# Another order of the seven down products, with one token half complete after the fifth

## The chip, the cores and the metric

One core of a Trainium2 chip. The engines named below are TensorE (PE), VectorE (DVE), ScalarE (ACT), GpSimd (POOL) and SyncE (SP), which here issues nearly all DMA transfers. The metric is the device time of one execution in microseconds.

## The reference, cut to what matters

Two layers on 1024 tokens of 1024 features (FF width 2816). Each layer is a mixer, a layer norm, a SwiGLU feed-forward and another layer norm:

```
def layer_norm(x, g, b):
    xf = x.astype(jnp.float32)
    mu = jnp.mean(xf, -1, keepdims=True)
    var = jnp.mean(jnp.square(xf - mu), -1, keepdims=True)
    return ((xf - mu) * lax.rsqrt(var + LN_EPS)).astype(x.dtype) * g + b

def swiglu(x, w_gate, w_up, w_down):
    return (jax.nn.silu(x @ w_gate) * (x @ w_up)) @ w_down
...
        x = layer_norm(ALPHA * x + mix, ln_mix_g[l], ln_mix_b[l])
        x = layer_norm(ALPHA * x + swiglu(x, ffn_w_gate[l], ffn_w_up[l], ffn_w_down[l]),
                       ln_ffn_g[l], ln_ffn_b[l])
```

The mixer of layer 0 is attention, that of layer 1 retention and a spatial-gating MLP; its first step (`gate`) multiplies the transposed output of layer 0 by a weight slice.

## The kernel before

**Matrix products in seven.** Each large product of the feed-forward is cut in two along tokens, features and the inner dimension, and done with seven half-size products in place of eight, on sums and differences of the blocks. For the down projection, product i (1 to 7) multiplies operand `h_ops[i-1]`, which the gate/up stage has stored to DRAM, by a block of `ffn_w_down` (i = 1, 2, 4) or by a stored combination `d_ops` (i = 3, 5, 6, 7). The results are added into `y[0]` and `y[1]`, the rows of the two token halves (4 row blocks of 128 tokens each, 1024 features in two column halves `ca` and `cb`). In the order of the kernel before: product 1 begins half 0, `ca`; 2 completes that; 6 and 5 begin half 1 (`ca`, `cb`); 7 completes half 1, `cb`, and begins half 0, `cb`; 3 completes half 1, `ca`; 4 completes half 0, `cb`. Products 1, 6, 7, 4 use one set of four PSUM banks (`side` true), 2, 5, 3 another, of which two banks come from the pool `trp` that the transposes use too.

**Precision.** Each operand tile is split into a rounded high part (a cast on ACT, L66) and a remainder (a subtraction on DVE, L67), and each 128x128 by 128x512 step is three matmuls (high by high, high by low, low by high). A product has 11 inner steps k, 4 row blocks b4 and 3 passes, 132 matmuls; a layer's down stage 924. Products run k by k over all row blocks, but the last one (i = 4) runs row block by row block after its first k.

**Buffers.** Operands come through four raw buffers of 512 KB (`load_raw`, `raw_h` and `raw_d`), h tiles through a pool of 11, weights through `w_unit`: unit `turn[0] % n` is one of eight tiles of the lasting pool `wpool`, or, from 8 on, a tile of an extra pool: four (`fw`) in the gate/up stage, six (`fww`) in the down stage. The pools of the down stage use the memory that the gate/up stage's pools (`c0`, `fw`) leave, so a tile in them waits until those have been read for the last time.

**Order.** The kernel is scheduled by its framework's list scheduler, which decides the order of each engine's queue; only the mixers' PE order is written out. Each engine, and SP's queue, works in order.

**After the products.** `sum_up` adds a product's PSUM to `y`; when a row block is complete `rows_done` normalises it, stores it (`scratch`, or `out` in layer 1) and, in layer 0, transposes it (`row_to_x`, L148) and splits it into the next layer's operand `xn`: with `pe` the remainder is made by a matmul with the negative identity and a copy on ACT (L153, L154), else by a subtraction on DVE (L156). `layer_norm` with `act` normalises on ACT (L174), multiplies on DVE (L175) and adds on POOL (L176); else two instructions on DVE do it (L178, L179). The reciprocal root is a pow on POOL (L166). The sums are L1040 and L1044; `zps` (L127) is the gate's product, `oq0ps` (L117) the first product behind it, `bw_u` (L872) the last product of gate/up, and `cy` and `c0` the results there, stored by L1009.

Of the kernel before, what the change touches and what calls it, by code (L numbers as in the profile page):

```python
# [11 lines left out]
F32 = mybir.dt.float32  # L12
# [6 lines left out]
P = 128  # L19
# [3 lines left out]
NB = SEQ // P  # L23
# [12 lines left out]
def tile_trunk(  # L36
# [7 lines left out]
    V, A, G, T, S = nc.vector, nc.scalar, nc.gpsimd, nc.tensor, nc.sync  # L44
# [5 lines left out]
    small = ctx.enter_context(tc.tile_pool(name="small", bufs=4))  # L50
# [19 lines left out]
    turn = [0, 0]  # L70
# [84 lines left out]
        else:  # L155
            V.tensor_sub(xt[:, :, 1, sl], ps, xt[:, :, 0, sl].bitcast(F32))  # L156

    def ln_stats(src, n, name):
        st = small.tile([P, n, 6], F32, tag="st", name=f"st_{name}")
        for j in range(n):  # L160
            V.bn_stats(st[:, j], src[:, j * 512:(j + 1) * 512])
        mv = small.tile([P, 2], F32, tag="mv", name=f"mv_{name}")
        V.bn_aggr(mv, st.rearrange("p a b -> p (a b)"))
        rstd = small.tile([P, 1], F32, tag="rstd", name=f"rstd_{name}")
        V.tensor_scalar_add(rstd, mv[:, 1:2], EPS)
        G.tensor_tensor(rstd, rstd, nhalf[:, 0:1], op=ALU.pow)  # L166
        return mv, rstd

    def layer_norm(row, gb, n, name, act=False):
        mv, rstd = ln_stats(row, n, name)  # L170
        if act:
            nm = small.tile([P, 1], F32, tag="c", name=f"nm_{name}")
            V.scalar_tensor_tensor(nm, mv[:, 0:1], -1.0, rstd, op0=ALU.mult, op1=ALU.mult)
            A.activation(row, row, AF.Identity, bias=nm, scale=rstd)  # L174
            V.tensor_mul(row, row, gb[0])  # L175
            G.tensor_add(row, row, gb[1])  # L176
        else:
            V.scalar_tensor_tensor(row, row, mv[:, 0:1], gb[0], op0=ALU.subtract, op1=ALU.mult)  # L178
            V.scalar_tensor_tensor(row, row, rstd, gb[1], op0=ALU.mult, op1=ALU.add)  # L179
# [444 lines left out]
    def odd_mixer(xT, zw0, res):  # L624
        with ExitStack() as st:
# [38 lines left out]
            def gate():  # L664

                zw = [zw0, col2_w(w_in, 2304, "zv1")]
                for g in (0, 1):
                    for t in range(NB):
                        ps = mm_tile("zps")
                        yield from gemm_R(ps[:, :256], zw[g], xT[t // 4], t % 4)  # L670
                        if g == 0:
                            A.copy(zv[:, t, :256], ps[:, :256])
                        else:
                            A.activation(zv[:, t, 256:], ps[:, :256], AF.Gelu_apprx_tanh)
                            A.activation(zv[:, t, :256], zv[:, t, :256], AF.Gelu_apprx_tanh)
                            layer_norm(zv[:, t], lngb, 1, f"sgu{t}")
                        yield 0.33
# [172 lines left out]
    def rest(layer, op, ahead=None):  # L850
# [7 lines left out]
        with ExitStack() as st:  # L858
# [156 lines left out]
            with ExitStack() as sl:  # L1015
# [7 lines left out]
                d_src = {1: wd[:, 0, :, ca], 2: wd[:, 1, :, ca], 4: wd[:, 1, :, cb], 6: d_ops[0][:, :, ca],  # L1023
                         7: d_ops[0][:, :, cb], 3: d_ops[1][:, :, ca], 5: d_ops[1][:, :, cb]}

                def rows_done(h, b4):
                    yt = y[h][:, b4]
                    t = 4 * h + b4
                    layer_norm(yt, gb, 2, f"f{layer}{h}{b4}")
                    if last:  # L1030
                        S.dma_start(out[0, t * P:(t + 1) * P, :], yt)
                    else:
                        S.dma_start(scratch[t], yt)
                        for c in (0, 1):
                            row_to_x(yt[:, c * 512:(c + 1) * 512], xn[h][c], b4, trp, f"f{layer}{h}{b4}{c}")

                def sum_up(i, b4, ps):
                    def first(h, c):
                        yt = y[h][:, b4, c]
                        V.scalar_tensor_tensor(yt, yt, ALPHA, ps, op0=ALU.mult, op1=ALU.add)  # L1040

                    def more(h, c, op=V.tensor_add):
                        yt = y[h][:, b4, c]
                        op(yt, yt, ps)  # L1044

                    if i == 1:
                        first(0, ca)
                    elif i == 2:
                        more(0, ca)
                    elif i == 6:  # L1050
                        first(1, ca)
                    elif i == 5:
                        first(1, cb)
                    elif i == 7:
                        more(1, cb)
                        first(0, cb)
                    elif i == 3:
                        more(1, ca)
                        rows_done(1, b4)
                    else:  # L1060
                        more(0, cb, V.tensor_sub)
                        rows_done(0, b4)

                bank = {}
                for i in (1, 2, 6, 5, 7, 3, 4):
                    end = i == 4
                    if end and not last:
                        loaded = ahead()
                        turn[0] = 4
                    if i == 3 and not last:  # L1070
                        xn = new_x("xn")
                    hs, ds = [], []
                    for q in range(0, NP, 2):
# [33 lines left out]
                    else:  # L1107
# [2 lines left out]
                                part(k, b4)  # L1110
                        for b4 in range(4):
                            sum_up(i, b4, bank[side][b4])
                more_w.pop()
            more_r.pop()
            return None if last else (xn, loaded, scratch)
# [51 lines left out]
```

## Time and profile before

| | |
|---|---|
| time, median of 3 runs | 2332.98 us (2329.07 to 2333.74) |
| the profiled execution | 2331.5 us |
| its span | 2329.6 us |
| mean granted clock of PE | 0.989 |
| PE busy, share of the span | 97% |
| DVE, ACT, POOL busy | 65%, 39%, 5% |
| down-stage matmuls (`pd`, L1096) | 1848, 427.2 us busy |

The span is that of the profile, from the first instruction to the end of the last; the time of the execution is 1.9 us longer. Busy shares are means over the whole span; a place where an engine waits shows only in the waits, the windows and the timeline.

### The profile page before, as it was taken

The page shows a single profiled execution, that of the slowest core. Times are in us where ns is not written, and L with a number is a line of the kernel's source. Part 1 is how long each engine was busy: PE and PEld are TensorE (multiplying, and loading weights), DVE is VectorE, ACT ScalarE, POOL GpSimd, SP SyncE. Part 2 cuts the span into 40 slices and gives each one's busy share as a digit, 9 for nine tenths or more (in the row PEclk, how much of TensorE's full clock was granted, in tenths as well). Part 3 has the DMA queues.
Part 4 walks back from the last instruction along what each step waited for, and adds up shares of the span by engine and source line. Part 5 has one row for each costly group of instructions (what it writes and reads, how often), then busy time and mean ns, then how long its engine had stood idle before and what let it go on. Part 6 is the DMA issues. An engine that isn't in the chain of part 4 may idle for free.

```text
span 2329.6 us, 30375 instructions
## 1 busy us (share of the span) xinstructions
PE 2262.2 (97%) x11372; PEld 1881.6 (81%) x11372; DVE 1506.2 (65%) x3030; ACT 904.2 (39%) x1740; POOL 108.5 (5%) x103
## 2 busy tenths in 40 slices
PE   8999999999999999989998999999999999989997
PEld 6888888878788888868886988888788888877885
DVE  4767676777877667755558523446976766755557
ACT  4545455553543333334332321122543333334431
POOL 0000000001200000000002100001200000000001
PEclk9999999999999999999998999999999999999998
DMA  5212121224254545457555111144344445457553
GB/s 168 68 46 59 42 58 40 70 90 136 87 190 163 170 152 164 147 195 268 199 186 173 42 46 46 46 149 149 123 148 159 159 162 169 137 197 270 172 193 123
DMA packets 195538, 312.36 MB, mean 134 GB/s; under 512 B 14784, under 2 KB 98368, under 8 KB 195392
## 3 DMA queue, kind: packets, MB, share of 16 engines
q1 hardware_dynamic: 195392, 310.44, 40.5%
q8 instruction: 89, 1.46, 0.3%
q14 instruction: 57, 0.47, 0.1%
HBM read 218.64 MB, written 87.56 MB: 131 GB/s over the span
## 4 chain that ended last, share of the span: by engine, by line
PE 78%; DVE 11%; DMA 7%; ACT 2%; issue 2%; POOL 0%; SPq 0%; POOLq 0%; ACTq 0%; DVEq 0%
PE bx_g L872 8%; PE bx_u L872 7%; PE pd L1096 7%; PE bw_g L872 5%; PE bw_u L872 5%; PE vps L127 4%; PE qps L117 4%; PE kps L117 3%; PE po_o L231 3%; DMA raw_d<-d_ops 3%; PE bv_g L872 3%; PE bv_u L872 2%; PE bz_u L872 2%; PE bz_g L872 2%; PE zps L127 2%; PE ovps L127 2%
## 5 line engine op out<-in xcount | busy, mean ns | idle before, releaser
L1096 PE MATMUL pd<-w_d,h 128*128 128x512 f32 x1848 | 427.2, 394 | 19.9 <-ACT w_d L66 15.0
L1096 PEld LDWEIGHTS pd<-w_d,h 128*128 128x128 f32 x1848 | 351.1, 190 | 95.5 <-ACT w_d L66 15.9
L872 PE MATMUL bx_g<-xs,w_g 128*128 128x512 f32 x792 | 192.2, 390 | 0.6 <-ACT w_g L66 0.6
L872 PE MATMUL bx_u<-xs,w_u 128*128 128x512 f32 x792 | 190.9, 389 | 0.0
L67 DVE TENSOR_TENSOR w_d<-raw_d,w_d 128x512 fp32r<-128x512 f32 x154 | 100.4, 685 | 124.5 <-ACT w_d L66 124.4
L872 PEld LDWEIGHTS bx_g<-xs,w_g 128*128 128x128 f32 x792 | 148.2, 188 | 32.2 <-ACT w_g L66 0.8
L872 PEld LDWEIGHTS bx_u<-xs,w_u 128*128 128x128 f32 x792 | 148.6, 188 | 30.8
L66 ACT CAST w_d<-raw_d 128x512 fp32r<-128x512 f32 x154 | 88.7, 618 | 147.4 <-DMA raw_d<-d_ops 101.4
L67 DVE TENSOR_TENSOR h<-raw_h,h 128x512 fp32r<-128x512 f32 x154 | 102.5, 684 | 58.4 <-ACT h L66 58.4
L872 PE MATMUL bw_u<-xs,w_u 128*128 128x512 f32 x528 | 130.9, 390 | 3.4 <-DVE cy L923 3.4
L872 PE MATMUL bw_g<-xs,w_g 128*128 128x512 f32 x528 | 130.7, 389 | 0.0
L66 ACT CAST h<-raw_h 128x512 fp32r<-128x512 f32 x154 | 91.6, 618 | 93.2 <-DMA raw_h<-h_ops 92.4
L872 PEld LDWEIGHTS bw_u<-xs,w_u 128*128 128x128 f32 x528 | 99.0, 188 | 24.8 <-DVE cy L923 4.3
L437 ACT ACTIVATE s<-s,mx 128x640 f32<-128x640 f32 (+7 forms) x128 | 93.2, 731 | 65.4 <-DVE mx L435 65.0
L127 PE MATMUL vps<-w_v,x 128*128 128x256 f32 x768 | 115.0, 294 | 1.5 <-DVE k L337 1.5
L872 PEld LDWEIGHTS bw_g<-xs,w_g 128*128 128x128 f32 x528 | 99.0, 188 | 20.5
L117 PE MATMUL qps<-x,w_q 128*128 128x512 f32 x384 | 109.9, 408 | 0.9 <-ACT w_q L66 0.9
L117 PE MATMUL kps<-x,w_k 128*128 128x512 f32 x384 | 110.4, 408 | 0.0
L127 PEld LDWEIGHTS vps<-w_v,x 128*128 128x128 f32 x768 | 101.3, 194 | 6.5 <-issue 4.6
L66 ACT CAST w_u<-raw_u 128x512 fp32r<-128x512 f32 x118 | 73.2, 622 | 78.9 <-issue 41.5
L67 DVE TENSOR_TENSOR w_u<-raw_u,w_u 128x512 fp32r<-128x512 f32 x118 | 80.8, 686 | 35.6 <-ACT w_u L66 35.4
L66 ACT CAST w_g<-raw_g 128x512 fp32r<-128x512 f32 x110 | 68.3, 625 | 87.8 <-PE bw_g L872 37.5
(574 smaller groups left out, 4070.5 us busy)
## 6 DMA issues: line engine op xcount, KB each, us to landing
raw_h<-h_ops SPq DMA_DIRECT2D x70, 512.0 KB, 4.1
h_ops<-cy SPq DMA_DIRECT2D x110, 256.0 KB, 3.1
raw_g<-in_ffn_w_gate_dram SPq DMA_DIRECT2D x44, 512.0 KB, 4.5
raw_u<-in_ffn_w_up_dram SPq DMA_DIRECT2D x44, 512.0 KB, 5.1
raw_dr<-in_ffn_w_down_dram SPq DMA_DIRECT2D x44, 512.0 KB, 3.6
d_ops<-raw_dr SPq DMA_DIRECT2D x44, 512.0 KB, 2.7
raw_d<-d_ops SPq DMA_DIRECT2D x40, 512.0 KB, 5.0
raw_d<-in_ffn_w_down_dram SPq DMA_DIRECT2D x30, 512.0 KB, 4.7
```

Source lines behind the costliest of these rows:

```text
L66: A.copy(dst[:, 0], src)
L67: V.tensor_sub(dst[:, 1], src, dst[:, 0].bitcast(F32))
L117: T.matmul(ps, w[k // 4][:, a, (k % 4) * P:(k % 4 + 1) * P], xh[k // 4][:, k % 4, b, :], start=n == 0, stop=n == 3 * KT - 1)
L127: T.matmul(ps, xh[k // 4][:, k % 4, a, b4 * P:(b4 + 1) * P], ws[k // 2][:, b, (k % 2) * 256:(k % 2) * 256 + 256], start=n == 0, stop=n == ...
L231: T.matmul(ps, self.xo[h][c][:, k, a, b4 * P:(b4 + 1) * P], self.w[c][2 * nh + k // 2][k % 2][:, b], start=n == 0, stop=n == 11)
L437: A.activation(s[:, :L], s[:, :L], AF.Exp, bias=self.mx[:, m:m + 1], scale=0.125, accum_out=self.sm[:, m:m + 1])
L872: T.matmul(ps, w[:, a, k * P:(k + 1) * P], X[i][:, k, b, :], start=first and n == 0, stop=n == 11, skip_group_check=more or not first)
L1096: T.matmul(bank[side][b4], hs[k][:, a, b4 * P:(b4 + 1) * P], ds[k][:, b], start=fresh and k == 0 and n == 0, stop=k == NP - 1 and n == 2, ...
```

## The change

The seven down products run in the order 1, 5, 6, 3, 7, 2, 4. Half 1 is complete with the fifth of them (product 7), and its four row blocks are normalised after that product, with `act` and, in layer 0, transposed with `pe`. Half 0 is still complete with product 4, but its `ca` half already with product 2, so the first of its two `bn_stats` is taken there and copied later (`st0`). `turn[0]` is set to 0 ahead of the products, so that product 1 begins with the units of `wpool`. The gate of layer 1's mixer takes the row blocks of half 1 first.

```diff
@@ -155,9 +155,12 @@
         else:
             V.tensor_sub(xt[:, :, 1, sl], ps, xt[:, :, 0, sl].bitcast(F32))
 
-    def ln_stats(src, n, name):
-        st = small.tile([P, n, 6], F32, tag="st", name=f"st_{name}")
-        for j in range(n):
+    def ln_stats(src, n, name, st=None):
+
+        s0, st = st, small.tile([P, n, 6], F32, tag="st", name=f"st_{name}")
+        if s0 is not None:
+            V.tensor_copy(st[:, 0], s0)
+        for j in range(s0 is not None, n):
             V.bn_stats(st[:, j], src[:, j * 512:(j + 1) * 512])
         mv = small.tile([P, 2], F32, tag="mv", name=f"mv_{name}")
         V.bn_aggr(mv, st.rearrange("p a b -> p (a b)"))
@@ -166,8 +169,8 @@
         G.tensor_tensor(rstd, rstd, nhalf[:, 0:1], op=ALU.pow)
         return mv, rstd
 
-    def layer_norm(row, gb, n, name, act=False):
-        mv, rstd = ln_stats(row, n, name)
+    def layer_norm(row, gb, n, name, act=False, st=None):
+        mv, rstd = ln_stats(row, n, name, st)
         if act:
             nm = small.tile([P, 1], F32, tag="c", name=f"nm_{name}")
             V.scalar_tensor_tensor(nm, mv[:, 0:1], -1.0, rstd, op0=ALU.mult, op1=ALU.mult)
@@ -665,7 +668,7 @@
 
                 zw = [zw0, col2_w(w_in, 2304, "zv1")]
                 for g in (0, 1):
-                    for t in range(NB):
+                    for t in (4, 5, 6, 7, 0, 1, 2, 3):
                         ps = mm_tile("zps")
                         yield from gemm_R(ps[:, :256], zw[g], xT[t // 4], t % 4)
                         if g == 0:
@@ -1023,16 +1026,18 @@
                 d_src = {1: wd[:, 0, :, ca], 2: wd[:, 1, :, ca], 4: wd[:, 1, :, cb], 6: d_ops[0][:, :, ca],
                          7: d_ops[0][:, :, cb], 3: d_ops[1][:, :, ca], 5: d_ops[1][:, :, cb]}
 
+                st0 = {}
+
                 def rows_done(h, b4):
                     yt = y[h][:, b4]
                     t = 4 * h + b4
-                    layer_norm(yt, gb, 2, f"f{layer}{h}{b4}")
+                    layer_norm(yt, gb, 2, f"f{layer}{h}{b4}", act=h == 1, st=None if h else st0[b4])
                     if last:
                         S.dma_start(out[0, t * P:(t + 1) * P, :], yt)
                     else:
                         S.dma_start(scratch[t], yt)
                         for c in (0, 1):
-                            row_to_x(yt[:, c * 512:(c + 1) * 512], xn[h][c], b4, trp, f"f{layer}{h}{b4}{c}")
+                            row_to_x(yt[:, c * 512:(c + 1) * 512], xn[h][c], b4, trp, f"f{layer}{h}{b4}{c}", pe=h == 1)
 
                 def sum_up(i, b4, ps):
                     def first(h, c):
@@ -1045,29 +1050,31 @@
 
                     if i == 1:
                         first(0, ca)
-                    elif i == 2:
-                        more(0, ca)
+                    elif i == 5:
+                        first(1, cb)
                     elif i == 6:
                         first(1, ca)
-                    elif i == 5:
-                        first(1, cb)
+                    elif i == 3:
+                        more(1, ca)
                     elif i == 7:
                         more(1, cb)
                         first(0, cb)
-                    elif i == 3:
-                        more(1, ca)
-                        rows_done(1, b4)
+                    elif i == 2:
+                        more(0, ca)
+                        st0[b4] = small.tile([P, 6], F32, tag="s6", name=f"st0_{layer}_{b4}")
+                        V.bn_stats(st0[b4], y[0][:, b4, ca])
                     else:
                         more(0, cb, V.tensor_sub)
                         rows_done(0, b4)
 
                 bank = {}
-                for i in (1, 2, 6, 5, 7, 3, 4):
+                turn[0] = 0
+                for i in (1, 5, 6, 3, 7, 2, 4):
                     end = i == 4
                     if end and not last:
                         loaded = ahead()
                         turn[0] = 4
-                    if i == 3 and not last:
+                    if i == 7 and not last:
                         xn = new_x("xn")
                     hs, ds = [], []
                     for q in range(0, NP, 2):
@@ -1110,6 +1117,9 @@
                                 part(k, b4)
                         for b4 in range(4):
                             sum_up(i, b4, bank[side][b4])
+                        if i == 7:
+                            for b4 in range(4):
+                                rows_done(1, b4)
                 more_w.pop()
             more_r.pop()
             return None if last else (xn, loaded, scratch)
```

How the scheduler places it, at three places. In the rows `pd_0_1_2` is layer 0, product 1, row block 2; `w_d0_1_0` and `h0_1_0` are the weight and h tiles of its k = 0; a last number is only a counter, and `x3` counts matmuls.

PE at the seam of layer 0, from the last gate/up product to the first down product; before:

```order
L872 MATMUL bw_u0_10_9896<-xs0_5_6834,w_u0_10_5_9850 128x512 x2
L872 MATMUL bw_u0_10_9896<-xs0_3_6835,w_u0_10_3_9854 128x512 x12
L1096 MATMUL pd_0_1_0_10058<-w_d0_1_0_9975,h0_1_0_9972 128x512
L1096 MATMUL pd_0_1_1_10059<-w_d0_1_0_9975,h0_1_0_9972 128x512
L1096 MATMUL pd_0_1_2_10060<-w_d0_1_0_9975,h0_1_0_9972 128x512
```

and now:

```order
L875 MATMUL bw_u0_10_9896<-xs0_5_6834,w_u0_10_5_9850 128x512 x2
L1103 MATMUL pd_0_1_0_10058<-w_d0_1_0_9975,h0_1_0_9972 128x512 x3
L1103 MATMUL pd_0_1_1_10059<-w_d0_1_0_9975,h0_1_0_9972 128x512 x3
L1103 MATMUL pd_0_1_0_10058<-w_d0_1_1_9981,h0_1_1_9978 128x512 x3
L1103 MATMUL pd_0_1_1_10059<-w_d0_1_1_9981,h0_1_1_9978 128x512 x3
L1103 MATMUL pd_0_1_0_10058<-w_d0_1_2_9991,h0_1_2_9988 128x512 x3
L1103 MATMUL pd_0_1_1_10059<-w_d0_1_2_9991,h0_1_2_9988 128x512 x3
L1103 MATMUL pd_0_1_0_10058<-w_d0_1_3_9997,h0_1_3_9994 128x512 x3
L1103 MATMUL pd_0_1_2_10060<-w_d0_1_0_9975,h0_1_0_9972 128x512 x3
L1103 MATMUL pd_0_1_2_10060<-w_d0_1_1_9981,h0_1_1_9978 128x512 x2
L875 MATMUL bw_u0_10_9896<-xs0_3_6835,w_u0_10_3_9854 128x512 x12
```

The first 26 pd matmuls now stand ahead of the last twelve of `bw_u`. Layer 1's seam has the same order.

SP's queue at the same place, with the loads of product 1 (`raw_h`, `raw_d`), of the rows to be added to (`yf`) and the stores of gate/up; before:

```order
L1009 DMA h_ops0_6222<-cy_0_9_9384 128x512 x2
L1092 DMA yf_0_0_9966<-mix_rows0_6221 128x1024 x4
L1009 DMA h_ops0_6222<-c0_0_10_9666 128x512
L88 DMA raw_h0_1_4_10000<-h_ops0_6222 128x2x512
L88 DMA raw_d0_1_4_10002<-in_ffn_w_down_dram 128x2x512
L88 DMA raw_h0_1_6_10016<-h_ops0_6222 128x2x512
```

and now:

```order
L1012 DMA h_ops0_6222<-cy_0_9_9384 128x512 x2
L88 DMA raw_h0_1_4_10000<-h_ops0_6222 128x2x512
L1099 DMA yf_0_0_9966<-mix_rows0_6221 128x1024 x4
L88 DMA raw_d0_1_6_10018<-in_ffn_w_down_dram 128x2x512
L1012 DMA h_ops0_6222<-c0_0_10_9666 128x512
L88 DMA raw_d0_1_4_10002<-in_ffn_w_down_dram 128x2x512
L88 DMA raw_h0_1_6_10016<-h_ops0_6222 128x2x512
```

`raw_h0_1_4` moved from behind the four yf loads to ahead of them, and `raw_d0_1_6` up to right behind them. In layer 1 the yf loads stand behind most of product 1's own loads, as before.

PE at the transposes of half 1 in layer 0 (`xt_f01..`); before, they follow parts of product 4, most of them its end:

```order
L1096 MATMUL pd_0_4_3_11561<-w_d0_4_10_11555,h0_4_10_11552 128x512 x3
L148 MATMUL xt_f0110_11386<-ident_75,yf_0_1_9967 128x128 x4
L148 MATMUL xt_f0111_11393<-ident_75,yf_0_1_9967 128x128 x4
L148 MATMUL xt_f0120_11412<-ident_75,yf_0_1_9967 128x128 x4
L148 MATMUL xt_f0121_11419<-ident_75,yf_0_1_9967 128x128 x4
L148 MATMUL xt_f0130_11438<-ident_75,yf_0_1_9967 128x128 x4
```

and now they stand in product 2:

```order
L1103 MATMUL pd_0_2_1_11333<-w_d0_2_10_11329,h0_2_10_11326 128x512 x3
L148 MATMUL xt_f0100_11136<-ident_75,yf_0_1_9967 128x128 x4
L148 MATMUL xt_f0101_11144<-ident_75,yf_0_1_9967 128x128 x4
L153 MATMUL xt_f0100_11136<-xn_10_10890,nident_80 128x512
L153 MATMUL xt_f0101_11144<-xn_11_10891,nident_80 128x512
...
L148 MATMUL xt_f0130_11226<-ident_75,yf_0_1_9967 128x128 x4
L148 MATMUL xt_f0131_11234<-ident_75,yf_0_1_9967 128x128 x4
L153 MATMUL xt_f0130_11226<-xn_10_10890,nident_80 128x512
L153 MATMUL xt_f0131_11234<-xn_11_10891,nident_80 128x512
L1103 MATMUL pd_0_2_2_11334<-w_d0_2_0_11249,h0_2_0_11246 128x512 x3
```

Row blocks 0 and 1 of product 2 run through all k, then all 32 transposes and 8 matmuls for the low parts, and only then row blocks 2 and 3 begin.

## Rows read from the trace of the kernel before

**Rows 1.** Page, engines: busy us (share of the span), instructions.

```profile
PE 2262.2 (97%) x11372; PEld 1881.6 (81%) x11372; DVE 1506.2 (65%) x3030; ACT 904.2 (39%) x1740; POOL 108.5 (5%) x103
```

**Rows 2.** Waits of PE, 1000 to 1330 (layer 0): us, times, longest.

```profile
PE xt_f L148 <- DVE xn L156: 10.2, 4, 4.3
...
PE pd L1096 <- ACT w_d L66: 7.4, 1, 7.4
```

**Rows 3.** Waits of PE, 2050 to 2330 (layer 1).

```profile
PE pd L1096 <- ACT w_d L66: 7.6, 1, 7.6
...
PE pd L1096 <- DVE h L67: 4.5, 2, 3.9
```

**Rows 4.** Windows, layer 0: engines' busy us, then PEclk, DMA share, GB/s.

```profile
1045.46:1050.00 4.54, 4.54 (x13) 3.63 (x14) 3.82 (x7) 2.55 (x5) 0.00 (x0) 0.65 0.63 231
...
1050.00:1060.00 10.00, 10.00 (x45) 8.26 (x44) 0.69 (x1) 0.62 (x1) 0.00 (x0) 1.00 1.00 393
...
1050.00:1200.00 150.00, 150.00 (x663) 124.19 (x662) 80.80 (x130) 62.92 (x114) 0.00 (x0) 1.00 0.65 225
...
1264.00:1269.00 5.00, 1.12 (x4) 0.72 (x4) 5.00 (x8) 0.37 (x1) 2.16 (x2) 0.50 0.70 252
```

**Rows 5.** Windows, layer 1 (columns as before).

```profile
2295.30:2300.00 4.70, 4.70 (x11) 3.73 (x12) 4.70 (x11) 0.00 (x0) 2.28 (x2) 0.50 0.01 3
```

**Rows 6.** Timeline of ACT, layer 0's seam: start, us, instruction, idle before.

```profile
1044.79 2.70 ACT L66 CAST w_d<-raw_d 128x512 fp32r<-128x512 f32 x5 [0.53 <-DMA h_ops<-c]
```

**Rows 7.** Timeline of DVE, layer 1: product 4 and the tail.

```profile
2288.52 0.69 DVE L67 TENSOR_TENSOR w_d<-raw_d,w_d 128x512 fp32r<-128x512 f32 x1 [2.63 <-ACT w_d L66]
...
2294.61 0.63 DVE L67 TENSOR_TENSOR h<-raw_h,h 128x512 fp32r<-128x512 f32 x1
...
2319.69 0.68 DVE L1044 TENSOR_TENSOR yf<-yf,pd 128x512 f32<-128x512 f32 x1
...
2320.29 1.28 DVE L179 SCALAR_TENSOR_TENSOR yf<-yf,rstd_f,gb_ffn 128x1024 f32<-128x1024 f32 x1
...
2324.24 1.28 DVE L179 SCALAR_TENSOR_TENSOR yf<-yf,rstd_f,gb_ffn 128x1024 f32<-128x1024 f32 x1 [0.44 <-POOL rstd_f L166]
```

**Rows 8.** Timeline of SP, layer 0's seam.

```profile
1013.20 1.74 SPq L1092 DMA_DIRECT2D yf<-mix_rows  x4
...
1028.44 0.37 SPq L88 DMA_DIRECT2D raw_h<-h_ops  x1
```

**Rows 9.** Timeline of POOL: the mixer's norm of layer 0, the tail.

```profile
566.68 2.40 POOL L176 TENSOR_TENSOR ym<-ym,gb_mix 128x1024 f32<-128x1024 f32 x1 [1.01 <-DVE nm_m L173]
...
2322.75 1.46 POOL L166 TENSOR_TENSOR rstd_f<-rstd_f,nhalf 128x1 f32<-128x1 f32 x1 [2.57 <-DVE rstd_f L165]
```

**Rows 10.** Norm by ACT, DVE, POOL, by line: ns min/median/max, starts.

```profile
L174 ACT ACTIVATE ym<-ym,nm_m,rstd_m x8: 1243/1244/1254, 564.0 to 1628.9; 128x1024 f32<-128x1024 f32 x8
...
L175 DVE TENSOR_TENSOR ym<-ym,gb_mix x8: 1214/1226/2235, 565.3 to 1630.2; 128x1024 f32<-128x1024 f32 x8
...
L176 POOL TENSOR_TENSOR ym<-ym,gb_mix x8: 2392/2402/2411, 566.7 to 1631.5; 128x1024 f32<-128x1024 f32 x8
```

**Rows 11.** Timeline of DVE, the mixer's norm of layer 0.

```profile
567.93 2.23 DVE L175 TENSOR_TENSOR ym<-ym,gb_mix 128x1024 f32<-128x1024 f32 x1
```

**Rows 12.** Timeline of PE: seams, layer 0's gate, layer 1's product 4.

```profile
1033.49 0.61 PE L872 MATMUL bw_u<-xs,w_u 128*128 128x512 f32 x2
...
1285.73 38.88 PE L127 MATMUL zps<-w_zv,xn 128*128 128x256 f32 x322
...
1324.81 5.49 PE L117 MATMUL oq0ps<-xn,w_oq 128*128 128x512 f32 x23
...
2087.89 3.06 PE L872 MATMUL bw_u<-xs,w_u 128*128 128x512 f32 x12 [2.47 <-DVE cy L923]
...
2295.30 23.76 PE L1096 MATMUL pd<-w_d,h 128*128 128x512 f32 x91 [3.87 <-DVE h L67]
```

**Rows 13.** Timeline of ACT, layer 1, ahead of product 4.

```profile
2280.93 1.66 ACT L66 CAST w_d<-raw_d 128x512 fp32r<-128x512 f32 x3 [5.71 <-DMA raw_d<-in_ffn_w_down_dram]
```

## The prediction

> **What bounds the kernel now.** I read the page first: TensorE (PE) is busy 97% of the span [rows 1], so time can only come out of the few places where PE stands still or runs at the lower clock. The sum below is made against the profiled execution, 2331.5 us; the median of the runs shown is 1.5 above it. A change within 0.2% (4.7 us) cannot be told from none.
>
> The waits of PE name the places. Around layer 0's down stage: 7.4 us for ScalarE's cast of w_d, and four waits, 10.2 us, of the transposes for VectorE's subtraction of xn [rows 2]. Around layer 1's: 7.6 us for w_d, 4.5 us for VectorE's h [rows 3]. The windows show what follows a wait: a granted clock of 0.65 for 4.5 us after the first, and 0.50 (1.2 of 2.4 GHz) among the waits of layer 0's end and after those of layer 1's, where the dense stretch has 1.00 [rows 4, 5]. A gap of 4 to 7 us so costs itself and 2 to 3 us more.
>
> Why w_d is late at the seam (from the last gate/up product to the first down product): ScalarE started those casts at 1044.79, released by the store of c [rows 6]. The first weight units lie in the down stage's own pool, which takes over the memory of c0 and of the extra gate/up units; no w_d can be cast before the last of c0 is stored.
>
> Why h is late in layer 1: VectorE works in order. Its subtraction for w_d at 2288.52 had waited 2.63 us for ScalarE, then four sums, a split and four bn_stats ran, and the h that PE needed came at 2294.61 [rows 7]. At layer 0's end it is the same queue: VectorE is busy 5.00 of 5 us, with the norms of half 1 and the subtractions of both halves in it, and PE does 1.12 [rows 4].
>
> **The change, part by part.** PE's work is priced by the dense stretch: 663 matmuls in 150.00 us, 0.226 us each, 209.0 for the 924 of a down stage [rows 4].
>
> *turn[0] = 0.* The first eight units of product 1 now lie in wpool, which no store holds. They are cast ahead of the gate's last activations, and 26 pd matmuls (5.9 us) stand on PE ahead of the last 12 of bw_u, as the first pair of orders shows. Units 8 to 10 still wait for the stores: before, the casts let pd start 7.4 us after bw_u [rows 2]; now 70 matmuls on units 0 to 7, 15.8 us, lie between the two. That covers them; without the cover the 7.4 us would come back there. New in layer 0, on SP: raw_h_4 stood behind the four yf loads issued from 1013.20 and was issued at 1028.44, when its buffer came free [rows 8]. Now it stands ahead of them (second pair), so the 2 MB of yf start after 1028.4, just ahead of raw_d_6, raw_d_4 and raw_h_6. With those, raw_h_4 and a store it is 4.25 MB; at the 393 GB/s of the saturated stretch [rows 4] that is 11 to 12 us, until about 1040.5. The splits of what lands last, and a copy on ScalarE behind them, stand ahead of what releases the last bw_u. PE is through its 26 matmuls at 1039.8 and then waits some 3.5 us (2 to 7). In layer 1 the yf loads keep their place: 1 us there (0 to 2).
>
> *Half 1 after the fifth product, layer 0.* Count from T, that product's end. VectorE has 8 sums and 4 bn_stats, one each 0.60 us (the step from the sum at 2319.69 to the instruction at 2320.29, [rows 7]), 7.2; then the small ones, between them four pows of GpSimd of up to 1.46 [rows 9]. The first normalise may start near T+9.2. An ACTIVATE takes 1.244, a mul 1.226, an add 2.402 [rows 10]. The adds are the slowest: done at T+14.2, 16.6, 19.0 and 21.4. Per row follow 8 transposes, two casts, two matmuls for the low part and two casts; ScalarE's four at 0.54 (five in 2.70, [rows 6]) and PE's share bring the last row through at about T+25. Product 2's row blocks 2 and 3 stand behind these transposes on PE (third pair), since they take their two PSUM tiles. PE has 66 matmuls, 14.9 us, of the other blocks; from T+14.9 to T+25 it has only 5 to 6 us of work. About 4 us idle and 3 for the clock: 7 (4 to 11). In return the 10.2 us at the end fall: the gate starts with half 1, which is ready by then, and half 0's norm has one of its two bn_stats behind it. Four scratch stores, waiting for GpSimd's adds, now stand on SP ahead of most of product 4's loads, and ScalarE's casts of h for product 4 behind those of xn. What covers them is the rest of product 2, 15 us; I take 2.5 us (0 to 6) there, and 1.5 (0 to 3) in the gate.
>
> One pair of rows bears on the adds. A mul that takes 1.226 as a rule took 2.23 from 567.93, beside an add that ran from 566.68 for 2.40 [rows 9, 11]: it ended 1.1 us, nearly its own length, after the add. If all take turns so, four muls and four adds are 14.5 us in series, the last add ends at T+25.0 and not T+21.4, and the sum is 3.6 us higher (rival 1). By the Trainium skill ("SBUF — State Buffer", "Who interferes with whom") a VectorE instruction with two SBUF inputs and a GpSimd one that reads SBUF exclude each other for a whole instruction, which speaks against this change; the trace's 2.23 agrees, and what it would make of the time is rival 1.
>
> *Layer 0's sum.* From 1033.9, the end of bw_u x2 (two of 0.226 from 1033.49, [rows 12]): 12 matmuls 2.7, 924 are 209.0, 384 zps at 0.121 (322 in 38.88, [rows 12]) 46.4, 64 transposes, which are half as wide, 6.4 at 0.1 (7.7 at most), 8 matmuls for low parts 1.8, and 0.3 for four small transposes: 1300.5. With 3.5 + 7 + 2.5 + 1.5 of waits 1315.0. Before, the first matmul behind all this (oq0ps) started at 1324.81 [rows 12]: 9.8 gained (range -4 to +17).
>
> *Layer 1.* PE had ended bw_u x2 2.47 before 2087.89, at 2085.4 [rows 12]. With 2.7 + 209.0 this gives 2297.1. Nothing is transposed here; the wait to fear is the one in product 4, which runs row block 0 through all k first and so needs the last h early. Its inputs are no faster than before: ScalarE had waited 5.71 us for a transfer until 2280.93 [rows 13], and four raw buffers set that pace wherever PE stands. On VectorE the queue between the first sum and the last h has three sums and two bn_stats, where it had two more bn_stats and an aggregate, 1.3 us; ScalarE's four ACTIVATEs now stand in the middle of those casts. The bounds are no wait and all of the 4.5; I take 2 and 1.5 for the clock, nearer to none because norms no longer stand there. With 1 at the seam and 0.5 elsewhere PE ends at 2302.1; before, at 2319.1 (23.76 from 2295.30, [rows 12]).
>
> The tail: VectorE's last sum at 2319.69 was followed by 1.28 us for row 2 before row 3's bn_stats, and the last instruction started at 2324.24 [rows 7], and the span ends at 2329.6. Now a row block needs a sum, one bn_stats, small ones and two of 1.28 with 0.44 of waiting, under 5 us, and PE's 30 matmuls for it are 6.8: row 2 is done when row 3 comes. Some 9.0 from PE's end, where it was 10.5: 2311.1, 18.5 gained (range 10 to 23).
>
> *Sum.* 9.8 + 18.5 = 28.3 off 2331.5 is 2303.2; with part of the 1.5 to the median I say **2304**.
>
> **Rivals.**
> 1. *Muls and adds take turns* (0.13), as that one pair did: the adds' chain in layer 0 ends 3.6 us later, with it product 2: 2308. For it the 2.23; against it, that most of the eight muls took 1.23, since few met an add.
> 2. *The loads take back layer 1's early start* (0.16). PE reaches product 4 some 17 us earlier, the loads do not, and the waits for h come back doubled: 9 us with their clock beyond what I count, 2313. For it: 5.71 us of idle ScalarE, and h that was late already. Against it: before product 4 no pd waited for an h at all [rows 3].
> 3. *The seam's gap only moves* (0.09): PE waits at unit 8 for the stores, or the first casts wait for gate/up units still being read. Against it stand the 15.8 us of cover. Both gaps come back with their clock, 20 us: 2324.
> 4. *Slower: GpSimd's adds hold up layer 0* (0.06). They release product 2's PSUM tiles and, on SP, product 4's loads. For it: 2.40 an add, 2.23 a mul. It decides once it eats 28 us; to be 5 us slower than before, 2337, the last add would have to end 33 us later than counted, at T+54. Against it: one after the other all eight end at T+25.
> 5. *Better* (0.06): other work covers the chain in product 2, and h is in time: 2304 - 14 = 2290.
>
> **How the numbers follow.** The forecast has 0.50, and by its own bounds 2296 to 2310. The range takes in rivals 1 and 2, and of 5 the nearer half: 2291 to 2319, leaving out rivals 3 and 4. Faster are all but rival 4 and a little of unknown costs: 0.90; same 0.04; slower 0.06.
>
> **What the profile after would show.** If right: no wait of pd for w_d of more than 2 us at either seam; bw_u's last 12 behind pd matmuls, after a wait of 2 to 7 us in layer 0; in layer 0's product 2 a stretch of 10 us with PE about half busy, the transposes waiting for GpSimd's add; no long wait for xn in the gate; some 9 us from the last matmul to the end. It is wrong if pd waits for w_d of unit 8 (rival 3), for h or w_d in layer 1's product 4 by more than 5 us (rival 2), or if the stretch in product 2 is over 20 us (rival 4).

## The result, and the profile after

| | before | after |
|---|---|---|
| median (lowest to highest), us | 2333.36 (2329.07 to 2341.12) | 2306.95 (2304.41 to 2311.05) |
| profiled execution, us | 2331.5 | 2308.59 |
| its span, us | 2329.6 | 2306.8 |
| mean granted clock of PE | 0.989 | 0.994 |

The ratio is 0.9885, with an interval of 0.9854 to 0.9915: faster by 26.4 us, and 3 us above the 2304 that was forecast. The total hides two errors of opposite sign, so the stages come first. Each is cut out of one profiled execution by rows of PE's timeline. Layer 0's stage runs from the end of the last `bw_u` pair to the first `oq0ps`, layer 1's from the same pair to the end of the last `pd`, the tail from there to the end of the span. PE's own work is by the prediction's prices: 266.6 in layer 0 (its 1300.5 less 1033.9), 211.7 in layer 1 (2.7 + 209.0).

| us | before | after | gained | forecast |
|---|---|---|---|---|
| layer 0's stage | 290.9 | 274.4 | 16.5 | 9.8 |
| layer 1's stage and tail | 233.8 + 10.5 | 225.5 + 8.5 | 10.3 | 18.5 |
| all that lies outside | 794.4 | 798.4 | -4.0 | 0 |

The sum is 22.8, the difference of the two spans. Of the 4.0 outside, 1.5 lies ahead of layer 0's stage. A second profiled execution of the changed kernel (below) had 2.9 less of it, so this part is scatter.

Two lines of the page of the kernel after; behind the bars of the second stand busy us, mean ns of one, and the idle time before with what ended most of it:

```profile
span 2306.8 us, 30426 instructions
...
L1103 PE MATMUL pd<-w_d,h 128*128 128x512 f32 x1848 | 425.0, 392 | 8.5 <-DVE h L67 5.3
```

The waits of PE in layer 0, 1000 to 1330, which answer to [rows 2] (us, times, longest):

```profile
PE xt_f L148 <- POOL yf L179: 2.0, 2, 1.0
PE xt_f L153 <- ACT xn L151: 0.9, 4, 0.2
...
```

And in layer 1, 2030 to 2310, which answer to [rows 3]:

```profile
PE pd L1103 <- DVE h L67: 5.3, 4, 2.5
PE pd L1103 <- ACT h L66: 3.0, 1, 3.0
```

Both waits for w_d, 7.4 and 7.6 us, are gone, and so are the four for VectorE's xn. New in layer 0 are small ones for GpSimd and for ScalarE's casts, 3.4 us with the two of 0.2 and 0.3 not shown. In layer 1 the wait for h has grown from 4.8 us (the 4.5 of [rows 3] and 0.3 for ScalarE's cast) to 8.3.

Layer 0's seam on PE's timeline (start, us, instruction):

```profile
1035.00 0.62 PE L875 MATMUL bw_u<-xs,w_u 128*128 128x512 f32 x2
1035.46 6.06 PE L1103 MATMUL pd<-w_d,h 128*128 128x512 f32 x26
1041.35 2.88 PE L875 MATMUL bw_u<-xs,w_u 128*128 128x512 f32 x12
1044.07 31.21 PE L1103 MATMUL pd<-w_d,h 128*128 128x512 f32 x137
```

The 26 `pd` stand ahead of the last 12 of `bw_u`, as counted, and no row has an idle time. The two loads to compare with [rows 8], on SP's timeline:

```profile
1012.61 0.37 SPq L88 DMA_DIRECT2D raw_h<-h_ops  x1
1014.85 1.80 SPq L1099 DMA_DIRECT2D yf<-mix_rows  x4
```

raw_h_4 is issued at 1012.61 and not at 1028.44, and the yf loads start behind it at 1014.85. The jam of transfers that the prediction priced at 3.5 us did not form. What let the load go shows on VectorE: this row ends at 1012.58, so by the times the raw buffer that came free was that of a weight.

```profile
1011.89 0.69 DVE L67 TENSOR_TENSOR w_d<-raw_d,w_d 128x512 fp32r<-128x512 f32 x1 [0.61 <-ACT w_d L66]
```

Layer 0's product 2 on PE (a bracket is the idle time ahead of the group and what ended it):

```profile
1202.85 1.09 PE L148 MATMUL xt_f<-ident,yf 128*128 128x128 f32 x8
...
1206.15 1.09 PE L148 MATMUL xt_f<-ident,yf 128*128 128x128 f32 x8 [0.98 <-POOL yf L179]
1207.48 0.99 PE L153 MATMUL xt_f<-xn,nident 128*128 128x512 f32 x2 [0.24 <-ACT xn L151]
...
1214.55 41.37 PE L1103 MATMUL pd<-w_d,h 128*128 128x512 f32 x181 [0.19 <-ACT xn L154]
...
1309.87 10.48 PE L117 MATMUL oq0ps<-xn,w_oq 128*128 128x512 f32 x45
```

The stretch holds 32 transposes and 8 low-part matmuls, 5.0 us at the prediction's prices (32 x 0.1 + 8 x 0.226), and takes 11.7: 6.7 lost where 7 was counted. Half of it, 3.4, is idle time ahead of the groups. Most of the rest stands inside them: the second low-part matmul of a pair waits for the second of ScalarE's two casts, so that a pair takes 0.99 where the dense pitch gives 0.45. The waits of its weight loads show this (PEld, 1202 to 1215):

```profile
PEld xt_f L153 <- ACT xn L151: 3.1, 8, 0.5
```

The transposes of the four row blocks start at 1202.85, 1206.15, 1209.46 and 1212.07: the first three are 3.3 us apart.

What GpSimd's four adds do meanwhile, in both layers:

```profile
1199.54 12.19 POOL L179 TENSOR_TENSOR yf<-yf,gb_ffn 128x1024 f32<-128x1024 f32 x4 [1.46 <-issue]
...
2248.60 15.02 POOL L179 TENSOR_TENSOR yf<-yf,gb_ffn 128x1024 f32<-128x1024 f32 x4 [1.76 <-issue]
```

On the mean they are 3.05 and 3.75 us each, in place of 2.40 [rows 10]. In layer 0 three of them take 3.3 us, the pace of the transposes, and the last one 2.36; in layer 1 the first takes 6.65, beside muls and subtractions. VectorE beside them:

```profile
1198.19 8.99 DVE L178 TENSOR_TENSOR yf<-yf,gb_ffn 128x1024 f32<-128x1024 f32 x4
L178 DVE TENSOR_TENSOR yf<-yf,gb_ffn x4: 1218/2298/3423, 1198.2 to 1203.8; 128x1024 f32<-128x1024 f32 x4
...
2253.83 7.58 DVE L67 TENSOR_TENSOR w_d<-raw_d,w_d 128x512 fp32r<-128x512 f32 x3 [0.84 <-ACT w_d L66]
2261.34 2.83 DVE L67 TENSOR_TENSOR h<-raw_h,h 128x512 fp32r<-128x512 f32 x1
2264.09 0.68 DVE L67 TENSOR_TENSOR w_d<-raw_d,w_d 128x512 fp32r<-128x512 f32 x1
```

The second line is layer 0's four muls again, with the shortest, median and longest in ns: two take 1.22 us, as in [rows 10], and the two that stand between adds 3.4. In layer 1 a subtraction of 0.69 takes 2.0 to 2.9 while the adds run, and 0.68 again as soon as they have ended, at 2263.6. In these rows VectorE and GpSimd take turns. What follows on ScalarE and PE in layer 1, first the cast that waits longest:

```profile
2268.44 0.62 ACT L66 CAST w_d<-raw_d 128x512 fp32r<-128x512 f32 x1 [7.60 <-DMA raw_d<-in_ffn_w_down_dram]
```

Windows of layer 1's product 4 (columns of [rows 4]):

```profile
2264.20:2274.60 10.40, 4.56 (x12) 2.29 (x12) 7.29 (x14) 1.66 (x3) 0.00 (x0) 0.79 0.23 77
2274.60:2279.00 4.40, 4.38 (x10) 3.47 (x11) 4.28 (x11) 0.00 (x0) 1.06 (x1) 0.50 0.00 0
2279.00:2284.00 5.00, 5.00 (x20) 4.03 (x19) 1.28 (x1) 0.00 (x0) 0.40 (x1) 0.86 0.26 105
```

After the waits the granted clock is 0.50 (1.2 of 2.4 GHz). By the dense pitch the 42 matmuls of the three windows are 9.5 us; they are busy for 13.9, 4.4 more. With the 8.3 of waits that is 12.7 of the 13.8 us that layer 1 loses over its 211.7.

### The profile page after: what moved, and what is told of

It is laid out like the page before. It is cut to its first block, busy times and chain, and to the rows that moved or that the text cites. A ratio compares the mean times of both kernels' runs of the same rounds, so it can differ in the third digit from the quotient of the medians.

```text
span 2306.8 us, 30426 instructions
## 1 busy us (share of the span) xinstructions
PE 2263.5 (98%) x11380; PEld 1882.4 (82%) x11380; DVE 1509.3 (65%) x3030; ACT 917.9 (40%) x1756; POOL 128.6 (6%) x111
## 5 line engine op out<-in xcount | busy, mean ns | idle before, releaser
L67 DVE TENSOR_TENSOR w_d<-raw_d,w_d 128x512 fp32r<-128x512 f32 x154 | 106.6, 725 | 109.6 <-ACT w_d L66 109.3
L875 PEld LDWEIGHTS bw_g<-xs,w_g 128*128 128x128 f32 x528 | 99.0, 188 | 20.5
```

The costliest lines, as they stand in the source:

```text
L67: V.tensor_sub(dst[:, 1], src, dst[:, 0].bitcast(F32))
L875: T.matmul(ps, w[:, a, k * P:(k + 1) * P], X[i][:, k, b, :], start=first and n == 0, stop=n == 11, skip_group_check=more or not first)
```

## The experiments

Medians are of four executions, ratios against the kernel before on the same chip with their 95% interval; stage times are of one profiled execution each. The scheduler lays out every version anew, so a run can differ from its neighbour in more of the order than the lines shown.

**The changed kernel again**, as a base.

> The changed kernel once more, beside the others on one chip. Its earlier times scatter over 2304 to 2311, those with the add on VectorE in both layers over 2295 to 2298. If the taking of turns of GpSimd and VectorE falls out differently from run to run, the scatter shows again (some 6 us) and the median stays at 2305 to 2308.

2305.51 us (2304.01 to 2308.11), 0.9885 [0.987, 0.99]. Layer 0 275.1, layer 1 224.0 + 8.5, PE's waits there 3.8 and 2.5. The stages repeat within 1.5 us; outside them it took 795.5. The expectation's reason for the scatter does not hold: the four adds take 12.17 us in layer 0 and 15.05 in layer 1, as in the first execution (12.19 and 15.02).

**turn[0] = 0 alone**, in the kernel before:

```diff
+                turn[0] = 0
                 for i in (1, 2, 6, 5, 7, 3, 4):
```

> The kernel before with the one line turn[0] = 0 ahead of the products; old order, old norm. By the prediction's steps the two seam gaps go (7.4 and 7.6 us with 2 to 3 each for the clock), less what comes back: some 2316 if they are kept in full in both layers. If the loads take back layer 1's early start (rival 2), the wait for h in product 4 grows there from 4.8 us by 5 to 9: about 2321 to 2324. If the change gains only with its new order: within 5 us of 2333.

2307.37 us (2305.82 to 2308.66), 0.99 [0.9886, 0.9915]: one line has the whole gain that a measurement can tell. It is 22 us on this chip, where some 17 were expected. PE's waits in its layer 0:

```profile
PE xt_f L148 <- DVE xn L156: 7.5, 4, 3.2
PE xt_f L148 <- DVE rstd_f L165: 1.1, 1, 1.1
PE zps L127 <- ACT xn L151: 0.7, 1, 0.7
PE pd L1097 <- DVE w_d L67: 0.4, 1, 0.4
```

No wait for w_d is left at the seam but 0.4; the waits for xn at the end stay. Layer 0 is 282.0, and layer 1 214.0 + 13.4 with one wait for h, of 1.4: the wait in product 4 shrank where rival 2 has it grow. raw_h_4 goes out at 1013.03 here, so the line alone moves it. So the new order is worth 7 to 7.6 us in layer 0 (274.4 and 275.1 against 282.0), and in layer 1 the rest of the change costs 5.1 to 6.6 (232.5 and 234.0 against 227.4). The two cancel.

**The change without that line:**

```diff
-                turn[0] = 0
                 for i in (1, 5, 6, 3, 7, 2, 4):
```

> The changed kernel without turn[0] = 0. If that line is what closes the seams, both gaps of some 7.5 us with their clock are back: 20 to 22 us above the changed kernel, near 2328, and raw_h_4 is issued late again (about 1028), because raw_d_0 and raw_d_2 hold their raw buffers until the weight pool is free. If the new order alone moves pd ahead of bw_u's end: less than 5 us above it.

2349.93 us (2344.38 to 2351.37), 1.0069 [1.0047, 1.0091]: slower than before, by 17 us; I had expected it near 2328. So the line is worth 44 us in the new order and 22 in the old: the parts do not add up. The waits of PE in its layer 0 show that more than the seam came back:

```profile
PE xt_f L148 <- POOL yf L179: 7.9, 1, 7.9
PE pd L1102 <- ACT w_d L66: 7.1, 1, 7.1
PE xt_f L148 <- DVE yf L182: 3.2, 1, 3.2
PE zps L127 <- DVE yf L1049: 2.4, 1, 2.4
PE pd L1102 <- DVE h L67: 1.9, 1, 1.9
```

Layer 0 is 303.9 and layer 1 240.2 + 8.6, with 6.4 for w_d again and 7.6 for h. Its window of product 2 has PE at work for 20.5 of 34 us at a clock of 0.75:

```profile
1205.00:1239.00 34.00, 20.49 (x91) 15.07 (x91) 24.99 (x39) 15.82 (x25) 14.24 (x8) 0.75 0.30 112
```

Its SP also tells where the seam's load was late from. This is the same raw_h as above:

```profile
1013.07 1.74 SPq L1098 DMA_DIRECT2D yf<-mix_rows  x4
...
1028.25 0.37 SPq L88 DMA_DIRECT2D raw_h<-h_ops  x1
```

1028.25 without the line, 1012.61 with it. Without it the load goes out behind the second of these four subtractions of h, 0.6 us apart, which end the use of another raw buffer:

```profile
1026.93 2.50 DVE L67 TENSOR_TENSOR h<-raw_h,h 128x512 fp32r<-128x512 f32 x4 [3.17 <-ACT h L66]
```

Until then the raw buffers ahead of it hold weights that cannot be cast into the waiting pool (their casts start at 1044.36), and the line that frees the cast frees the buffer too.

**The add of half 1's norm on VectorE in layer 1:**

```diff
-            G.tensor_add(row, row, gb[1])
+            (adder or G).tensor_add(row, row, gb[1])
...
-                    layer_norm(yt, gb, 2, f"f{layer}{h}{b4}", act=h == 1, st=None if h else st0[b4])
+                    layer_norm(yt, gb, 2, f"f{layer}{h}{b4}", act=h == 1, st=None if h else st0[b4], adder=V if last else G)
```

> The changed kernel with the add of half 1's norm in layer 1 moved from GpSimd to VectorE (4 instructions); the rest as it is. In the changed kernel product 4 of layer 1 waited 8.3 us for h; four adds took 15.0 us there and VectorE's splits beside them 2.5 to 2.8 us in place of 0.69. Theory A (GpSimd's adds and VectorE's two-input splits take turns, the late splits hold the raw buffers): splits back at 0.69, last raw_d of product 4 issued some 4 us earlier, the waits for h fall to 3 to 5 us, the time by 4 to 6 us to about 2302. Theory B (four raw buffers set the pace of the loads, whoever splits): the waits stay at 7 to 9 us, the time within 2 us of 2307.

2300.28 us (2296.41 to 2304.74), 0.9865 [0.9848, 0.9881]. Theory A holds in each of its signs. The waits of PE in layer 1 fall from 8.3 (6.3 in the second execution) to 3.3:

```profile
PE pd L1103 <- DVE w_d L67: 2.0, 1, 2.0
PE pd L1103 <- ACT w_d L66: 1.3, 1, 1.3
```

Layer 1's stage falls from 225.5 (224.0) to 217.8, and the subtractions are back at 0.69:

```profile
2260.82 1.29 DVE L67 TENSOR_TENSOR w_d<-raw_d,w_d 128x512 fp32r<-128x512 f32 x2
```

The last load of product 4 shows the way from the one to the other. In the kernel after, SP waits 4.1 us for a subtraction of h to free the raw buffer, then issues it; the last row is the same load here:

```profile
SPq L88 <- DVE h L67: 4.1, 1, 4.1
2265.40 0.33 SPq L88 DMA_DIRECT2D raw_d<-in_ffn_w_down_dram  x1
...
2265.08 0.34 SPq L88 DMA_DIRECT2D raw_d<-in_ffn_w_down_dram  x1
```

Counted from the start of the stage (2072.75 and 2076.07) that is 192.7 and 189.0, 3.6 us sooner. Another way would be that the stores of the rows, which wait for the adds, hold up the loads behind them on SP. But the two loads of h that stand behind such stores go out equally late in both, 183.0 and 185.9 against 183.1 and 185.5.

Layer 0's code is unchanged here, yet its profiled execution shows one wait of 4.7 us for GpSimd's add, and a clock of 0.76 in the stretch behind it:

```profile
1207.66 1.97 PE L148 MATMUL xt_f<-ident,yf 128*128 128x128 f32 x8 [4.68 <-POOL yf L179]
...
1219.36 41.34 PE L1103 MATMUL pd<-w_d,h 128*128 128x512 f32 x181 [0.19 <-ACT xn L154]
```

```profile
1207.60:1219.40 11.80, 10.61 (x41) 6.57 (x41) 9.04 (x8) 8.65 (x16) 8.94 (x4) 0.76 0.44 178
```

Layer 0 is 279.1 there, 4.7 more than in the profile of the kernel after. That is the wait alone: the stretch takes 11.70 us (1207.66 to 1219.36), as in the kernel after at a clock of 1.00, so here the lower clock cost nothing. Nor were the adds slower:

```profile
1188.43 1.15 ACT L66 CAST w_d<-raw_d 128x512 fp32r<-128x512 f32 x2 [7.04 <-DMA raw_d<-in_ffn_w_down_dram]
...
1204.40 12.14 POOL L179 TENSOR_TENSOR yf<-yf,gb_ffn 128x1024 f32<-128x1024 f32 x4 [1.46 <-issue]
```

They take 12.14 us and start 4.86 later. By that much, too, ScalarE's cast of a weight of product 2 is later (1183.57 in the kernel after), which waits for a transfer, and its subtraction stands on VectorE ahead of the sums of half 1. Why the transfers ran behind in this execution is open.

**The same in both layers** (`adder=V`):

> As the run before it, with the add on VectorE in layer 0 too. If the taking of turns also sets layer 0's chain in product 2 (four adds 12.2 us, four muls 9.0 us, where 9.6 and 4.9 were the lone prices): mul and add of all four rows are done some 3 to 4 us earlier, the stretch with transposes shrinks from 11.7 to about 8 us, and the time is 3 to 4 us below the run before it. If ScalarE's casts and PE's own chain set the stretch: unchanged within 1 us.

2296.23 us (2295.05 to 2297.58), 0.9853 [0.9838, 0.9868]; layer 0 272.5, layer 1 217.5 + 8.8. The stretch in product 2 takes 10.0 us (1203.19 to 1213.16), where about 8 was expected; its transposes start 2.5 us apart. Against the base's 0.9885 [0.987, 0.99] the intervals just don't meet: GpSimd's part of the norm costs some 7 us by the ratios, 9 by the medians.

**Half 1's norm left out in layer 1** (the kernel computes less; one execution):

```diff
+                    if not (last and h == 1):
+                        layer_norm(yt, gb, 2, f"f{layer}{h}{b4}", act=h == 1, st=None if h else st0[b4])
```

> Leaves out the norm of half 1 in layer 1 altogether (its rows are stored without it), to see the loads of product 4 alone. Theory A (the norm's adds hold up the splits): product 4 waits 2 us or less for h and w_d. Theory B (the loads' own pace): 7 to 9 us as before; in between, the difference is the norm's share.

2299.07 us; layer 1 219.2 + 8.9, with 3.4 of waits for h. This lies between the two theories, nearer to A. No norm at all leaves as much as a norm with its add on VectorE, so beyond GpSimd's adds the norm shows no cost in these two. It is not a floor: the last run below has the norm on VectorE alone and a wait of 0.7, so the order of the queues sets part of what is left.

**A fifth raw buffer in the down stage**, for one weight buffer, on top of `adder=V`:

```diff
-                more_w.append((sl.enter_context(tc.tile_pool(name=f"fww{layer}", bufs=6)), 6))
+                more_w.append((sl.enter_context(tc.tile_pool(name=f"fww{layer}", bufs=5)), 5))
+                more_r.append((sl.enter_context(tc.tile_pool(name=f"frd{layer}", bufs=1)), 1))
...
```

> The version with the add on VectorE in both layers (2296.2), with a fifth raw buffer in the down stage, paid for with one weight unit (five in the extra pool in place of six). In layer 1 that version still waits 2.9 us for w_d in product 4. If four raw buffers set the pace of the loads (rival 2): these waits go, 2 to 5 us faster. If the order of the splits on VectorE or the h tiles (free only when product 2 has read them) set it: within 1.5 us.

2301.93 us (2301.4 to 2303.92), 0.987 [0.9855, 0.9885]. PE waits for nothing in layer 1, 212.3 + 8.9, but layer 0 is 284.2: its transposes wait 4.0 for VectorE's yf and 3.5 for xn. So, in layer 1 alone (`nw = 5 if last else 6`):

> The add on VectorE in both layers (2296.2), with the fifth raw buffer (and five weight units in the extra pool) in layer 1 alone. With it in both layers layer 1's down stage lost its waits and took 221.2 us from the end of bw_u x2 to the end, where it was 226.3; layer 0's became 11.7 us longer, as the order there came out differently. If the two layers are independent: about 2291, layer 0 as before at 272 to 273 us. If the gain of layer 1 came from elsewhere: 2295 to 2298.

2292.37 us (2291.48 to 2295.0), 0.9838 [0.9822, 0.9854]. Layer 1's down stage on PE is then one row:

```profile
2077.26 204.16 PE L1106 MATMUL pd<-w_d,h 128*128 128x512 f32 x900
```

**That with layer 1 in the old order** and its old norm:

```diff
-                for i in (1, 5, 6, 3, 7, 2, 4):
+                for i in ((1, 2, 6, 5, 7, 3, 4) if last else (1, 5, 6, 3, 7, 2, 4)):
...
-                        if i == 7:
+                        if i == 7 and not last:
```

> As the run before it, but layer 1 with the order of products and the norm of the kernel before (1, 2, 6, 5, 7, 3, 4; VectorE alone). With turn[0] = 0 alone the old order had taken 227.4 us in layer 1, the new one 226.3 without GpSimd's adds. If the new order gives layer 1 next to nothing: within 2 us of the run before it. If half 1's norm is hidden there by the new order: 4 to 6 us slower, with waits for h in product 4.

2293.84 us (2291.77 to 2294.48), 0.9841 [0.9825, 0.9857]; no wait in layer 1, 212.3 + 10.0. Of the new order layer 1 has 1.1 us, in the tail.

**The old order of the gate**, on top of `adder=V` (`for t in range(NB):`):

> The version with the add on VectorE in both layers (2296.2), with the gate's row blocks in the old order, 0 to 7. If the gate's order is what hides the norm of half 0 behind the last product: 5 to 8 us slower, with waits of zps or the transposes for xn in the gate. If the early norm of half 1 alone does it: within 1.5 us.

2297.38 us (2296.09 to 2302.84), 0.9853 [0.9835, 0.9871]; layer 0 272.2 beside 272.5. Which half the gate starts with is worth nothing.

**Half 1's rows one product later**, behind product 2, on top of `adder=V`:

```diff
-                        if i == 7:
+                        if i == 2:
```

> The add on VectorE in both layers (2296.2), new order, but the rows of half 1 are normalised after product 2 (the sixth) in place of after product 7 (the fifth). If layer 0 gains because half 1 is out of the way before the last product: that stage goes from 272.5 us back to some 280, the time to 2302 to 2306. If the transposes standing in product 2 cost what the early norm gives: within 2 us.

2292.18 us (2291.51 to 2295.83), 0.9841 [0.9821, 0.986]. I had expected layer 0 near 280; it is 267.5, 0.9 over PE's own work, and PE waits nowhere in it. The edit did not do what the expectation says, though. The scheduler leaves half 1's norm where it was, VectorE's first add starting at 1200.80 (1199.81 in `adder=V`), and moves only the transposes, from 1203.19 to 1224.11, where they stand between matmuls of the products:

```profile
1200.80 1.22 DVE L179 TENSOR_TENSOR yf<-yf,gb_ffn 128x1024 f32<-128x1024 f32 x1
...
1224.11 1.03 PE L148 MATMUL xt_f<-ident,yf 128*128 128x128 f32 x8
1224.90 4.81 PE L1103 MATMUL pd<-w_d,h 128*128 128x512 f32 x20
1229.55 0.39 PE L153 MATMUL xt_f<-xn,nident 128*128 128x512 f32 x1
```

So the early transposes cost layer 0 some 5 us; whether the early norm gains anything, this run does not tell.

**Half 1's norm on VectorE alone**, as the other half's (`act=False`):

> The changed kernel with half 1's norm on VectorE alone (two instructions of 1.28 us a row in place of ScalarE's, VectorE's and GpSimd's). If GpSimd's part is all that the division of the norm costs: as the run with the add on VectorE (2296 to 2298). If ScalarE's part is worth something: 2 to 4 us slower than that; either way below the changed kernel's 2305 to 2307.

2295.02 us (2292.14 to 2296.48), 0.9846 [0.983, 0.9863]; layer 0 272.5, layer 1 213.5 + 8.9 with one wait of 0.7. Beside 217.5 with ScalarE's part that is 4 us less in layer 1, and by the medians no more time than `adder=V`: the split over ScalarE and GpSimd brings nothing.

## Why the prediction was right, and where it was not

The time, the sign and the first of its mechanisms held. The sums for the two layers were off by 7 and 8 us, in opposite directions; that the total came within 3 us is luck.

**turn[0] = 0 closes both seams: right.** No `pd` waits for w_d, the 15.8 us of cover were enough, and rival 3 is out. This line alone gives 0.99.

**Layer 0's seam wait of 3.5 us: wrong, it is 0.** The failed step is that raw_h_4 would still be issued at 1028.4, now with the yf loads behind it. That time was no property of the load: it was late because of the stall that the line removes, as the runs with and without the line show (1012.61 and 1013.03, against 1028.25 and 1028.44).

**Product 2, 7 us: 6.7 measured**, but not as 4 idle and 3 of clock. In the profile after, the clock stayed at 1.00, 3.4 is idle time and most of the rest is waiting for ScalarE's casts inside the groups. Behind another run's wait of 4.7 us the clock did fall to 0.76, and the stretch was no longer for it. **Rival 1's mechanism is the true one**: with T the end of product 7, 1187.9, and 1199.54 + 12.19 for the adds, the last one ended at 1211.7, T+23.8, where the sum had T+21.4 and turns in strict series T+25.0. Its price was smaller than the 3.6 given to it: the adds end 2.4 later than summed, and the stretch got 1.7 us shorter in the profile with the add on VectorE (11.7 to 10.0). **2.5 for products 2 to 4 and 1.5 for the gate: too much.** 274.4 less 266.6 and 6.7 leaves 1.1 for both. Of the reasons given for the gain at the end, the gate's order is worth nothing by its run.

**Layer 1, 5.0 us of waits and clock: 13.8 measured.** This is the sign that rival 2 was to show, h late by more than 5 us in product 4, and its 9 us beyond the sum fits the size (8.8). But its reason fell: with turn[0] = 0 alone PE reaches product 4's late h almost as early, in the old order (its wait begins 191.7 us into the stage, 2269.99 less 2078.30; 189.0 in the kernel after, 2261.72 less 2072.75), and waits 1.4. The step that failed is "nearer to none because norms no longer stand there". The norms had moved a product ahead, where their adds made VectorE's subtractions 2.0 to 2.9 us long. The add on VectorE takes 7.7 us off the stage (6.2 against the second execution). Late subtractions keep the raw buffers, so the last load comes late, by the 4.1 us that SP waits for it; the fifth buffer removes what is left, 217.5 to 212.3. The clock, counted at 1.5, cost 4.4 by the windows. The prediction had weighed the adds against the muls in layer 0 alone, and not against the splits that share their time in layer 1. By the Trainium skill ("SBUF — State Buffer", "Who interferes with whom") a VectorE instruction with two SBUF inputs and a GpSimd one that reads SBUF exclude each other; these rows agree (2.0 to 2.9 us in place of 0.69).

**The tail, 9.0: 8.5**, right, for the reason given.

**What stays open.** What gives layer 0 its 7 us in the new order: the waits for VectorE's xn are gone, but the early norm, the low parts made on PE and half 0's early statistics were not run apart; the gate's order and the norm's split over the engines are worth nothing by their runs. Why the run without turn[0] = 0 places layer 0's product 2 so badly, and why a fifth raw buffer costs layer 0 some 12 us, is seen only as another order of the queues. In the former, VectorE's sums of half 1 stand behind a subtraction of the gate's weights that waits 3.9 us for its cast. Rows behind product 2 and a fifth buffer in layer 1 were not tried together; by the stages, 267.5 and 221.2 in place of 272.5 and 226.3, an estimate is 10 us less than 2296.23.

## What to carry to other kernels

A load that is issued late may be late because of the very stall you remove: ask who holds its buffer before you price it as a new jam. Work moved off a busy VectorE to GpSimd is paid twice where VectorE has instructions with two inputs from SBUF to do at that time; list all of those in the stretch, not the ones beside it in the code. When a change has several parts, run each alone and the whole without it, since here one line carried the gain, the rest gave in one layer what it took in the other, and without the line the rest lost 17 us. And look in the trace whether an edit moved what it was meant to move.

## What the hardware showed that was not expected

A very small instruction can lose a whole add's time. VectorE's copy of 128 x 6 beside the last of GpSimd's adds, which ended at 1211.73 (ns min/median/max, first and last start):

```profile
L162 DVE COPY st_f<-st x2: 158/1214/2270, 1209.5 to 1211.7; 128x6 f32<-128x6 f32 x2
```

One took 2.27 us and ended with the add, the next 0.16. Not every instruction pays: between 1207.10 and 1209.57, while the adds ran, two sums with one input in PSUM and two bn_stats kept their 0.6 us each. And the turns repeat: the same four muls and four adds of layer 0 took 8.9 to 9.0 and 12.1 to 12.2 us in all five profiles that have them; where PE waited 4.7 us more, they only started later.
